# Norm weights that ride behind x transposed, ScalarE's first transfer, and two transfers for the first query weights

## The chip, the cores and the metric

One core of a Trainium2 chip runs the kernel once. The metric is the device time of one execution in microseconds (us). The kernel before has a median of 731.11 us in three runs (730.77 to 731.98).

## The reference

The kernel computes one decoder block on x of 512 tokens by 1,024 features in float32. The part that the change touches is the start: the norm of the input and the first projections.

```
h = x * rsqrt(mean(x*x) + EPS) * pre_mix_norm
[q_r, k_r, v_r, g_r, q_s, k_s, v_s, gate_r, gate_s] = h @ w_in
y_r = (silu(g_r) * GroupNorm(Retention_chunkwise(q_r, k_r, v_r))) @ w_ret_out
y_s = SWA_GQA_sinks_ALiBi(q_s, k_s, v_s) @ w_swa_out
x += RMSNorm((sigmoid(gate_r) * y_r + sigmoid(gate_s) * y_s) @ w_out) * post_mix_norm
x += RMSNorm(relu(RMSNorm(x) * pre_mlp_norm @ w_up)^2 @ w_down) * post_mlp_norm
```

## The kernel before

Every float32 matrix product is made of three products of rounded parts (`mm3`, lines 173 to 175): high by high, high by low, low by high. So each operand is split first: `split` (lines 129 and 130) writes the high part on ScalarE (ACT) and the rest on VectorE (DVE). TensorE (PE) does nothing but matmuls, 4,438 of them, in program order.

The start runs over KD = 8 blocks of 128 features. For each block k a transfer brings x transposed, `xTs[:, k]`, 128 partitions by 512 tokens, and another brings `raw_kv[:, k]`, the 256 columns of `w_in` that make sliding-window keys and values. `split_scaled` (lines 334 and 335) multiplies `xTs[:, k]` by the norm weight `gT[:, k]` of each feature and splits it into `xg`; `split` makes `wkv` of `raw_kv`. Then 12 matmuls per block add to four PSUM banks, `ptok`. The factor 1/rms of each token isn't known yet; it is put in later, as a row `R` (`factor_rows`, line 383 on PE and 385 on ACT), made of the squares of `xt`, x in its natural layout (line 354).

After the eight blocks come four `project_block`s of 24 matmuls each, with `pblk` as output: the sliding-window queries. Two of them use the weights of `raw_q` (a transfer of 1 MB, line 324), two those of a second pair (line 145). In the middle of the second block PE makes `R`. Then DVE scales the queries (line 408), makes the normed input out of `xTs`, `gT` and `R` (line 360), and ACT and DVE split it into `hT` (line 363 by way of `split`). The next `project_block` takes `hT` and the weights of `load_qk(0)`, two transfers of 512 KB in rows of 512 B (line 153): the retention queries and keys of head 0.

The order of work on each engine is set by a scheduler when the program is built; each engine then runs its own list strictly in order. Transfers are issued from three queues: SP's (`nc.sync`), ACT's (`nc.scalar`) and POOL's (`nc.gpsimd`, for transfers that add into a tile). SP's queue carries nearly all of the start. ACT's queue carries two: `gT` (128 partitions by 8 numbers) and `raw_kv` of block 0. In the list of ACT the split of `wkv` for block 1 stands ahead of that for block 0. `raw` tiles come from a ring of two buffers, so `raw_q` must be read before the transfers of `load_qk(0)` are issued.

Of the kernel before, what the change touches and what calls it, by code (L numbers as in the profile page):

```python
# [10 lines left out]
F32 = mybir.dt.float32  # L11
# [5 lines left out]
P = 128  # L17
D_MODEL = 1024
SEQ = 512
NT = SEQ // P  # L20
KD = D_MODEL // P
# [17 lines left out]
C_QR, C_KR, C_VR, C_GR, C_QS, C_KS, C_GATE_R = (0, 512, 1024, 2048, 3072, 3584, 3840)  # L39
# [47 lines left out]
    return np.ascontiguousarray(w.reshape(2, 4, P, 2, 512).transpose(3, 0, 2, 1, 4))  # L87


def f(ap):  # L90
    return ap.bitcast(F32)


@with_exitstack
def block_kernel(ctx, tc, x, xT, pre_mix, w_in, w_v, w_g, w_gate, w_ret, w_swa, w_out, sinks, post_mix,
                 pre_mlp, w_up, w_down, post_mlp, decay, chunk, dist, out):
    nc = tc.nc
    x, out = x[0], out[0]
    w_in, w_ret, w_swa, w_out = (w[0] for w in (w_in, w_ret, w_swa, w_out))
# [27 lines left out]
    def split(hi, lo, src):  # L127

        last["hi"] = nc.scalar.copy(hi, src)  # L129
        last["split"] = nc.vector.tensor_tensor(lo, src, f(hi), op=ALU.subtract)  # L130

    def raw_tile(shape):
        return stream.tile(shape, F32, name="raw", tag="raw", bufs=2)
# [49 lines left out]
    def wino_tokens(wx, b11, b12, b21, b22, f, dst):  # L183

        f11, f12, f21, f22 = f
        nc.vector.tensor_tensor(f11, f11, f12, op=ALU.subtract)
        split(dst[0][:, 0], dst[1][:, 0], f11)
        nc.vector.tensor_tensor(f12, f22, f12, op=ALU.subtract)
        split(dst[0][:, 2], dst[1][:, 2], f12)

        nc.vector.scalar_tensor_tensor(f22, f22, -1.0, f11, op0=ALU.mult, op1=ALU.subtract)
        split(dst[0][:, 1], dst[1][:, 1], f22)
        nc.vector.scalar_tensor_tensor(f21, f22, -1.0, f21, op0=ALU.mult, op1=ALU.subtract)
        split(dst[0][:, 3], dst[1][:, 3], f21)
        sums = [tuple(d[:, i] for d in dst) for i in range(4)]
        return {"11": b11, "21": b21, "22": b22, "t1": sums[0], "t2": sums[1],
                "t3": sums[2], "t4": sums[3]}
# [104 lines left out]
    side = ctx.enter_context(tc.tile_pool(name="side", bufs=1, side="right"))  # L302
    side.tile([P, 72], F32, name="pad")
    xTpool = sctx.enter_context(tc.tile_pool(name="xTpool", bufs=1, side="right"))
    xTs = xTpool.tile([P, KD, SEQ], F32, name="xTs", tag="xs")
    xgctx = ExitStack()
    xgpool = xgctx.enter_context(tc.tile_pool(name="xgpool", bufs=1, side="right"))
    gT = xgpool.tile([P, KD], F32, name="gT")
    xg = [xgpool.tile([P, KD, SEQ], F32R, name=f"xg{i}") for i in range(2)]
    xctx = ExitStack()  # L310
    xpool = xctx.enter_context(tc.tile_pool(name="xpool", bufs=1))
# [3 lines left out]
    nc.vector.memset(ones, 1.0)  # L315
    raw_kv = raw_tile([P, KD, 256])
    for k in range(KD):
        nc.sync.dma_start(xTs[:, k], xT[k])
        if k == 0:
            nc.scalar.dma_start(gT, pre_mix)  # L320
        queue = nc.scalar if k == 0 else nc.sync
        queue.dma_start(raw_kv[:, k], w_in[k * P : (k + 1) * P, C_KS : C_KS + 256])
    raw_q = raw_tile([P, KD, 256])
    nc.sync.dma_start(raw_q, w_in[:, C_QS : C_QS + 256].rearrange("(k p) c -> p k c", p=P))
    xts = [xpool.tile([P, D_MODEL], F32, name="xt", bufs=NT) for _ in range(NT)]
    for t in range(NT):
        nc.sync.dma_start(xts[t], x[t * P : (t + 1) * P, :])
# [4 lines left out]
    def split_scaled(hi, lo, src, scale):  # L332

        nc.scalar.mul(hi, src, scale)
        nc.vector.scalar_tensor_tensor(lo, src, scale, f(hi), op0=ALU.mult, op1=ALU.subtract)
# [620 lines left out]
    for half in range(2):  # L956
# [11 lines left out]
        with tc.high_priority(offset=CHAIN_AHEAD):  # L968
            for t in range(2):
# [4 lines left out]
                for n in range(2):  # L974
                    c = slice(n * 512, (n + 1) * 512)
# [152 lines left out]
    def left(j, q):  # L1128
        hi, lo = (ring.tile([P, 4, 256], F32R, name=f"left{i}") for i in range(2))
        split(hi, lo, uc[j][:, q])  # L1130
        return hi, lo

    def right(src):
        return [parts(src[:, 2 * i : 2 * i + 2], [P, 2, 512]) for i in range(2)]
# [141 lines left out]
    for j in range(2):  # L1276
        a, b = left(j, 3), right(tch[j])
# [21 lines left out]
    for i in range(2):  # L1299
        c = slice(i * 256, (i + 1) * 256)  # L1300
# [9 lines left out]
    residual(3, factor(3), [(512, outz[3])] + zs)  # L1310


_INS = ['x', 'xT', 'pre_mix_norm', 'w_in', 'w_v', 'w_g', 'w_gate', 'w_ret_out', 'w_swa_out', 'w_out', 'sinks', 'post_mix_norm',
        'pre_mlp_norm', 'w_up', 'w_down', 'post_mlp_norm']


# [28 lines left out]
```

## Time and profile before

| what | value |
|---|---|
| median of the runs shown | 731.11 us |
| the profiled execution's own time | 731.96 us |
| its span, first to last instruction | 730.2 us |
| PE busy | 718.1 us, 98% of the span |
| DVE busy | 535.6 us, 73% |
| ACT busy | 423.8 us, 58% |
| mean granted TensorE clock | 0.997 |
| bytes moved by transfers | 117.79 MB, 161 GB/s mean |

The profiled execution's time and its span differ by 1.8 us, which lies around the instructions. A row of a timeline gives the start, the duration, the engine, the line of the kernel, the operation, the output and inputs, and behind it in brackets how long the engine was idle before and what ended that. An engine name with a q (SPq, ACTq) marks the issue of a transfer, not the transfer.

### The profile page before, as it was taken

What the parts mean: (1) busy time and instruction counts of PE and PEld (TensorE: products, weight loads), DVE (VectorE), ACT (ScalarE), POOL (GpSimd) and SP (SyncE); (2) the same over time, 40 slices, a digit from 0 to 9 for tenths busy, and PEclk for the clock granted to TensorE, in tenths of its full rate; (3) what the DMA queues carried; (4) which work ended last, traced back from release to release, by engine and by line L of the source; (5) the groups of instructions that cost most, each with busy time, mean ns of one, the idle gap of its engine ahead of it and who ended that gap; (6) DMA issues with size and microseconds to landing.
All of it is one profiled execution on the core that took longest, in us unless ns stands there. A gap on an engine that the chain in (4) does not pass through costs nothing.

```text
span 730.2 us, 11250 instructions
## 1 busy us (share of the span) xinstructions
PE 718.1 (98%) x4438; PEld 640.3 (88%) x4438; DVE 535.6 (73%) x808; ACT 423.8 (58%) x714; POOL 60.5 (8%) x75
## 2 busy tenths in 40 slices
PE   8999999999999999999999999999999999999996
PEld 8877878888888999989888999999999888888885
DVE  5699976677975756566944866677676788987797
ACT  6667676445665534435634865766667756555571
POOL 0200000211100000000011101100000010010010
PEclk9999999999999999999999999999999999999998
DMA  9954434907444446543661619766753899698603
GB/s 314 331 170 85 104 83 144 289 4 145 87 144 117 143 117 179 151 133 115 216 247 58 160 49 283 198 172 169 197 147 117 266 291 238 156 203 200 116 0 116
DMA packets 43749, 117.79 MB, mean 161 GB/s; under 512 B 3504, under 2 KB 21296, under 8 KB 37552
## 3 DMA queue, kind: packets, MB, share of 16 engines
q1 hardware_dynamic: 36928, 80.76, 31.5%
q0 software_dynamic: 6480, 36.18, 26.4%
q8 instruction: 35, 0.57, 0.3%
q10 hardware_dynamic: 288, 0.14, 0.1%
q14 instruction: 18, 0.15, 0.1%
HBM read 114.96 MB, written 2.10 MB: 160 GB/s over the span
## 4 chain that ended last, share of the span: by engine, by line
PE 67%; DVE 5%; DMA 2%; issue 1%; ACT 1%; POOL 1%; POOLq 0%; DVEq 0%; ACTq 0%
PE wino L173 10%; PE wino L174 10%; PE wino L175 10%; PE p L174 5%; PE p L173 5%; PE p L175 5%; PE yr L173 2%; PE yr L174 2%; PE ps L174 2%; PE yr L175 2%; PE ps L175 2%; PE ps L173 2%; DVE wlo L130 2%; PE up L175 2%; PE up L174 2%; PE up L173 2%
## 5 line engine op out<-in xcount | busy, mean ns | idle before, releaser
L130 DVE TENSOR_TENSOR wlo<-raw,whi 128x1024 fp32r<-128x1024 f32 x81 | 98.6, 1222 | 49.6 <-ACT whi L129 49.6
L129 ACT CAST whi<-raw 128x1024 fp32r<-128x1024 f32 x81 | 84.7, 1051 | 41.4 <-DMA raw<-in_w_down 7.5
L174 PE MATMUL p<-wlo,left 128*128 128x512 f32 x216 | 84.2, 390 | 0.0
L175 PE MATMUL p<-whi,left 128*128 128x512 f32 x216 | 84.1, 390 | 0.0
L173 PE MATMUL p<-whi,left 128*128 128x512 f32 x216 | 84.0, 390 | 0.1
L175 PEld LDWEIGHTS p<-whi,left 128*128 128x128 f32 x216 | 40.5, 188 | 9.1 <-DVE left L130 0.8
L174 PEld LDWEIGHTS p<-wlo,left 128*128 128x128 f32 x216 | 40.6, 188 | 8.7 <-DVE wlo L130 0.3
L173 PEld LDWEIGHTS p<-whi,left 128*128 128x128 f32 x216 | 40.5, 188 | 8.8 <-ACT left L129 0.5
L130 DVE TENSOR_TENSOR wlo<-tch,whi 128x1024 fp32r<-128x1024 f32 x32 | 38.6, 1219 | 7.5 <-ACT whi L129 7.5
L129 ACT CAST left<-uc 128x1024 fp32r<-128x1024 f32 x28 | 29.3, 1052 | 23.2 <-PE p L174 23.2
L130 DVE TENSOR_TENSOR left<-uc,left 128x1024 fp32r<-128x1024 f32 x28 | 34.1, 1220 | 10.2 <-ACT left L129 10.2
L129 ACT CAST p<-rs 128x1024 fp32r<-128x1024 f32 x21 | 22.0, 1050 | 31.2 <-DVE rs L224 31.2
L129 ACT CAST whi<-tch 128x1024 fp32r<-128x1024 f32 x32 | 33.2, 1050 | 11.7 <-PE p L175 6.8
L130 DVE TENSOR_TENSOR p<-rs,p 128x1024 fp32r<-128x1024 f32 x21 | 25.7, 1225 | 14.7 <-ACT p L129 14.7
L130 DVE TENSOR_TENSOR wlo<-rs,whi 128x1024 fp32r<-128x1024 f32 x21 | 25.7, 1224 | 10.5 <-ACT whi L129 8.4
L173 PE MATMUL wino<-h2c,whi 128*128 128x256 f32 x104 | 29.4, 283 | 0.0
L174 PE MATMUL wino<-h2c,whi 128*128 128x256 f32 x104 | 29.4, 283 | 0.0
L175 PE MATMUL wino<-h2c,wlo 128*128 128x256 f32 x104 | 29.4, 283 | 0.0
L174 PE MATMUL wino<-h2s,p 128*128 128x256 f32 x104 | 29.4, 283 | 0.0
L175 PE MATMUL wino<-h2s,p 128*128 128x256 f32 x104 | 29.4, 283 | 0.0
L173 PE MATMUL wino<-h2s,whi 128*128 128x256 f32 x104 | 29.4, 283 | 0.0
L174 PE MATMUL wino<-h2s,whi 128*128 128x256 f32 x104 | 29.4, 283 | 0.0
(350 smaller groups left out, 2328.7 us busy)
## 6 DMA issues: line engine op xcount, KB each, us to landing
tch<-in_w_down POOLq DMA_DIRECT2D x12, 1024.0 KB, 9.6
raw<-in_w_down SPq DMA_DIRECT2D x7, 1024.0 KB, 7.6
rs<-in_w_up SPq DMA_DIRECT2D x13, 512.0 KB, 4.1
rs<-in_w_up POOLq DMA_DIRECT2D x13, 512.0 KB, 5.4
raw<-in_w_up SPq DMA_DIRECT2D x13, 512.0 KB, 5.1
raw<-in_w_in SPq DMA_DIRECT2D x8, 512.0 KB, 5.3
acc<-in_w_v POOLq DMA_DIRECT2D x4, 1024.0 KB, 8.0
rs<-in_w_gate SPq DMA_DIRECT2D x8, 512.0 KB, 3.7
```

The source lines that it names most:

```text
L129: last["hi"] = nc.scalar.copy(hi, src)
L130: last["split"] = nc.vector.tensor_tensor(lo, src, f(hi), op=ALU.subtract)
L173: nc.tensor.matmul(ps, ah, bh, start=first, stop=False, skip_group_check=more)
L174: nc.tensor.matmul(ps, ah, bl, start=False, stop=False, skip_group_check=more)
L175: nc.tensor.matmul(ps, al, bh, start=False, stop=last, skip_group_check=more)
```

## The change

Three edits, all in the first loads:

- The norm weights are no longer an input of their own. On the host each block of x transposed gets two more columns, both holding the norm weight of the feature, so a row is 514 numbers (2,056 B) where it was 512 (2,048 B). `xTs` and `gT` become views of the wider tile `xT_in`. The transfer of `gT` on ACT's queue is gone.
- With it gone, `raw_kv` of block 0 is the first and only transfer on ACT's queue.
- `raw_q` is loaded in two transfers of 128 columns each (rows of 512 B) where it was one transfer of 256 columns (rows of 1 KB).

```diff
+def norm_blocks(x, gain):
+
+    return np.concatenate([x.T, gain[:, None], gain[:, None]], 1).reshape(KD, P, SEQ + 2)
...
-    xTs = xTpool.tile([P, KD, SEQ], F32, name="xTs", tag="xs")
+
+    xT_in = xTpool.tile([P, KD, SEQ + 2], F32, name="xTs", tag="xs")
+    xTs = xT_in[:, :, :SEQ]
+    gT = xT_in[:, :, SEQ]
...
-    gT = xgpool.tile([P, KD], F32, name="gT")
...
     for k in range(KD):
-        nc.sync.dma_start(xTs[:, k], xT[k])
-        if k == 0:
-            nc.scalar.dma_start(gT, pre_mix)
+        nc.sync.dma_start(xT_in[:, k], xT[k])
         queue = nc.scalar if k == 0 else nc.sync
         queue.dma_start(raw_kv[:, k], w_in[k * P : (k + 1) * P, C_KS : C_KS + 256])
     raw_q = raw_tile([P, KD, 256])
-    nc.sync.dma_start(raw_q, w_in[:, C_QS : C_QS + 256].rearrange("(k p) c -> p k c", p=P))
+    for b in range(2):
+        c0 = C_QS + b * P
+        nc.sync.dma_start(
+            raw_q[:, :, b * P : (b + 1) * P],
+            w_in[:, c0 : c0 + P].rearrange("(k p) c -> p k c", p=P),
+        )
```

On ACT, at the very start, the list before is this (`raw_111` is `raw_kv`, `wkv0_108` and `xg0_102` are the high parts; a wait named DMAHW is one for a transfer):

```order
L320 DMA gT_101<-in_pre_mix_norm 128x8
L115 ACT_TABLE_LOAD
L115 ACTIVATE early_74<-mhalf_72 128x4 [waits DVE_49]
L322 DMA raw_111<-in_w_in 128x256
L334 ACTIVATE xg0_102<-xTs_97,gT_101 128x512 [waits DMAHW1_49,DMAHW0_49]
L334 ACTIVATE xg0_102<-xTs_97,gT_101 128x512 [waits DMAHW2_49]
L129 CAST wkv0_108<-raw_111 128x256 [waits DMAHW3_49]
L129 CAST wkv0_108<-raw_111 128x256 [waits DMAHW4_49]
```

Here the two `xg` of blocks 0 and 1 go ahead of the two `wkv`, and of these block 1 goes ahead of block 0. The list of the changed kernel at the same place:

```order
L327 DMA raw_110<-in_w_in 128x256
L120 ACT_TABLE_LOAD
L120 ACTIVATE early_74<-mhalf_72 128x4 [waits DVE_49]
L134 CAST wkv0_107<-raw_110 128x256 [waits DMAHW0_49]
L344 ACTIVATE xg0_101<-xTs_97 128x512 [waits DMAHW1_49]
L344 ACTIVATE xg0_101<-xTs_97 128x512 [waits DMAHW2_49]
L134 CAST wkv0_107<-raw_110 128x256 [waits DMAHW3_49]
```

The `wkv` split of block 0 has moved ahead of both `xg`, and that of block 1 stands behind them. DVE's list has the same shift: the low part of `wkv` for block 0 first, then two of `xg`, then block 1's.

On SP's queue the rows around `raw_q` before (`raw_129` is `raw_q`, `raw_405` the second pair of query weights, `acc_454` the retention values' weights, `raw_509` the weights of `load_qk(0)`):

```order
L324 DMA raw_129<-in_w_in 128x8x256
L327 DMA xt_131<-in_x 128x1024
L327 DMA xt_132<-in_x 128x1024
L327 DMA xt_133<-in_x 128x1024
L327 DMA xt_134<-in_x 128x1024
L145 DMA raw_405<-in_w_in 128x8x256
L597 DMA acc_454<-in_w_v 128x2048
L599 DMA acc_454<-in_w_v 128x2048
L153 DMA raw_509<-in_w_in 128x8x128 x2
```

And in the changed kernel:

```order
L331 DMA raw_127<-in_w_in 128x8x128 x2
L337 DMA xt_130<-in_x 128x1024
L337 DMA xt_131<-in_x 128x1024
L337 DMA xt_132<-in_x 128x1024
L337 DMA xt_133<-in_x 128x1024
L150 DMA raw_404<-in_w_in 128x8x256
L607 DMA acc_453<-in_w_v 128x2048
L609 DMA acc_453<-in_w_v 128x2048
L158 DMA raw_508<-in_w_in 128x8x128 x2
```

Only the first row differs, two transfers where one was; what follows keeps its order. PE's and POOL's lists are unchanged, and ACT's later list differs only in one `kv` copy (line 395) that now stands ahead of the last square of `xt`.

## Rows read from the trace of the kernel before

**Rows 1.** The longest waits of PE over the whole span: who waited for whom, us in total, times, longest.

```profile
PE ptok L173 <- ACT wkv L129: 1.5, 1, 1.5
PE warm L330 <- POOL ident masks.py:199: 1.4, 1, 1.4
PE pblk L175 <- DVE wlo L130: 0.8, 1, 0.8
PE swa_s L424 <- ACT vg L631: 0.7, 1, 0.7
```

**Rows 2.** Busy time by engine in the stretch from 3 to 33.5 us: length, busy us (instructions) of PE, PEld, DVE, ACT and POOL, granted clock, mean busy share of the 16 DMA engines, GB/s.

```profile
3.00:33.50 30.50, 28.92 (x176) 25.67 (x175) 19.01 (x34) 20.51 (x35) 5.14 (x9) 1.00 1.06 353
```

**Rows 3.** Timeline of ACT in the first 6 us, its issues of transfers among it.

```profile
0.74 0.40 ACTq L320 DMA_DIRECT2D gT<-in_pre_mix_norm  x1
1.24 0.39 ACTq L322 DMA_DIRECT2D raw<-in_w_in  x1
...
3.72 1.50 ACT L334 ACTIVATE xg<-xTs,gT 128x512 fp32r<-128x512 f32 x2 [1.05 <-DMA gT<-in_pre_mix_norm]
5.47 0.71 ACT L129 CAST wkv<-raw 128x256 fp32r<-128x256 f32 x2 [0.24 <-DMA raw<-in_w_in]
```

**Rows 4.** Timeline of DVE at the same place.

```profile
4.47 1.53 DVE L335 SCALAR_TENSOR_TENSOR xg<-xTs,gT,xg 128x512 fp32r<-128x512 f32 x2 [3.44 <-ACT xg L334]
6.21 0.76 DVE L130 TENSOR_TENSOR wkv<-raw,wkv 128x256 fp32r<-128x256 f32 x2 [0.20 <-ACT wkv L129]
```

**Rows 5.** Timeline of PE: the warm-up matmuls, the first three matmuls on data, the first of the first query block, and the eight that make R.

```profile
1.37 3.36 PE L330 MATMUL warm<-ident 128*128 128x128 f32 x14 [1.37 <-POOL ident masks.py:199]
6.23 0.38 PE L173 MATMUL ptok<-wkv,xg 128*128 128x256 f32 x1 [1.50 <-ACT wkv L129]
...
6.92 0.28 PE L175 MATMUL ptok<-wkv,xg 128*128 128x256 f32 x1
...
18.18 0.40 PE L173 MATMUL pblk<-xg,whi 128*128 128x512 f32 x1
...
26.59 1.05 PE L383 MATMUL R<-diag,ones 128*128 128x128 f32 x8
```

**Rows 6.** Issues on SP's queue: the first two blocks of x transposed, raw_kv of block 1, raw_q, and the two transfers of load_qk(0).

```profile
0.74 0.84 SPq L318 DMA_DIRECT2D xTs<-in_xT  x2
1.64 0.42 SPq L322 DMA_DIRECT2D raw<-in_w_in  x1
...
8.57 0.38 SPq L324 DMA_DIRECT2D raw<-in_w_in  x1
...
19.85 2.27 SPq L153 DMA_DIRECT2D raw<-in_w_in  x2
```

**Rows 7.** Issues with their size and the time from the start of the issue to the landing, each from a narrow stretch: block 0 of x transposed (issued at 0.74), raw_kv of block 0 (1.24) and of block 1 (1.64), raw_q (8.57), the first transfer of load_qk(0) (19.85).

```profile
xTs<-in_xT SPq DMA_DIRECT2D x1, 256.0 KB, 2.8
...
raw<-in_w_in ACTq DMA_DIRECT2D x1, 128.0 KB, 3.5
...
raw<-in_w_in SPq DMA_DIRECT2D x1, 128.0 KB, 3.8
...
raw<-in_w_in SPq DMA_DIRECT2D x1, 1024.0 KB, 7.8
...
raw<-in_w_in SPq DMA_DIRECT2D x1, 512.0 KB, 11.5
```

**Rows 8.** Packets in four stretches: 12.5 to 14.0 us (rows of 1 KB of raw_q, and three of 4 KB), 28.8 to 30.4 us (rows of 512 B of load_qk(0)), 16.5 to 18.5 us (rows of 4 KB of xt), and ACT's queue (q10) from 2.3 to 33.5 us: packets, MB, share of 16 engines. The smallest packets, counted under 512 B in the first three, are the marks that end a transfer.

```profile
DMA packets 517, 0.54 MB, mean 358 GB/s; under 512 B 2, under 2 KB 514, under 8 KB 517
...
DMA packets 929, 0.48 MB, mean 298 GB/s; under 512 B 14, under 2 KB 928, under 8 KB 928
...
DMA packets 221, 0.80 MB, mean 401 GB/s; under 512 B 28, under 2 KB 28, under 8 KB 220
...
q10 hardware_dynamic: 288, 0.14, 1.5%
```

**Rows 9.** Timeline of ACT from 31 to 36 us: the high parts of the weights of load_qk(0) (128x1024) and of the normed input hT (128x512).

```profile
31.39 1.05 ACT L129 CAST whi<-raw 128x1024 fp32r<-128x1024 f32 x1 [3.11 <-DMA raw<-in_w_in]
...
33.57 1.05 ACT L129 CAST whi<-raw 128x1024 fp32r<-128x1024 f32 x1 [0.62 <-DMA raw<-in_w_in]
34.53 1.14 ACT L129 CAST hT<-xTs 128x512 fp32r<-128x512 f32 x2
```

**Rows 10.** Timeline of DVE from 32 to 43.4 us; between the last two rows it has no idle time.

```profile
32.98 0.69 DVE L130 TENSOR_TENSOR hT<-xTs,hT 128x512 fp32r<-128x512 f32 x1 [0.97 <-ACT hT L129]
35.17 1.29 DVE L130 TENSOR_TENSOR hT<-xTs,hT 128x512 fp32r<-128x512 f32 x2 [1.50 <-ACT hT L129]
...
42.10 1.22 DVE L130 TENSOR_TENSOR wlo<-raw,whi 128x1024 fp32r<-128x1024 f32 x1
```

**Rows 11.** Timeline of PE at the first block on hT.

```profile
42.22 0.39 PE L174 MATMUL pblk<-hT,whi 128*128 128x512 f32 x1
43.37 0.50 PE L175 MATMUL pblk<-hT,wlo 128*128 128x512 f32 x1 [0.76 <-DVE wlo L130]
```

**Rows 12.** PE's last matmul, and the granted clock (the number ahead of the last two) in two stretches after it.

```profile
722.74 0.28 PE L175 MATMUL p4c<-whi,left 128*128 128x256 f32 x1
...
724.00:725.70 1.70, 0.00 (x0) 0.00 (x0) 0.84 (x3) 0.51 (x2) 0.55 (x1) 0.94 0.04 12
725.70:730.20 4.50, 0.00 (x0) 0.00 (x0) 1.35 (x3) 0.00 (x0) 0.00 (x0) 0.50 0.33 117
```

More of the change, by code (lines that the diff above doesn't have):

```diff
@@ L94, in block_kernel @@
 @with_exitstack
-def block_kernel(ctx, tc, x, xT, pre_mix, w_in, w_v, w_g, w_gate, w_ret, w_swa, w_out, sinks, post_mix,
+def block_kernel(ctx, tc, x, xT, w_in, w_v, w_g, w_gate, w_ret, w_swa, w_out, sinks, post_mix,
                  pre_mlp, w_up, w_down, post_mlp, decay, chunk, dist, out):
@@ L1310, in block_kernel @@
     residual(3, factor(3), [(512, outz[3])] + zs)
-_INS = ['x', 'xT', 'pre_mix_norm', 'w_in', 'w_v', 'w_g', 'w_gate', 'w_ret_out', 'w_swa_out', 'w_out', 'sinks', 'post_mix_norm',
+_INS = ['x', 'xT', 'w_in', 'w_v', 'w_g', 'w_gate', 'w_ret_out', 'w_swa_out', 'w_out', 'sinks', 'post_mix_norm',
         'pre_mlp_norm', 'w_up', 'w_down', 'post_mlp_norm']
@@ L1325 @@
         inputs, w_in=w_in[:, :, :C_GATE_R],
-        xT=np.asarray(inputs["x"])[0].T.reshape(KD, P, SEQ),
-        pre_mix_norm=np.asarray(inputs["pre_mix_norm"]).reshape(KD, P).T,
+        xT=norm_blocks(np.asarray(inputs["x"])[0], np.asarray(inputs["pre_mix_norm"])[0]),
         w_v=wide_blocks(w_in[0, :, C_VR:C_GR]),
```

## The prediction

> **What bounds the kernel now.** I began with PE's waits, since PE is busy for 98% of the span. The list is short [rows 1]: 1.5 us for the first matmul on data, 1.4 us for the warm-up's operand, 0.8 us for a weight split by DVE, 0.7 us for a copy by ACT, nothing longer. A gain at the start therefore lives only if none of the later waits takes it back, and the question is what ends each of them.
>
> The first wait: `ptok` starts at 6.23 [rows 5]. It needs `wkv` and `xg` of block 0. ACT makes the two `xg` first, from 3.72, when `gT` has landed, and then at 5.47 the first `wkv`, behind a transfer [rows 3]. That transfer is block 1's: it was issued at 1.64 [rows 6] and landed 3.8 us later [rows 7], at 5.44. Block 0's weights had landed at 1.24 + 3.5 = 4.74 [rows 3, 7], but their split stands second and ends at 5.47 + 0.71 = 6.18, just ahead of PE. PE then goes on without a break from its third matmul at 6.92 [rows 5].
>
> The third wait: PE's first block on `hT` issues two matmuls and stops; the third comes at 43.37, after 0.76 us idle, when DVE has written `wlo` at 42.10 + 1.22 = 43.32 [rows 10, 11]. Followed back, DVE has no idle time from 35.17 to there [rows 10], so its end is fixed at 35.17. At 35.17 it waited 1.50 us for ACT's `hT`; ACT makes that at 34.53, strictly behind a weight split that starts at 33.57, when the second transfer of `load_qk(0)` lands [rows 9]. And from 3 to 33.5 us the 16 DMA engines are full: share 1.06 at 353 GB/s [rows 2]. `load_qk(0)`'s first transfer was issued at 19.85 and landed 11.5 us later [rows 6, 7], most of which is queueing. So the chain that bounds this stage is the sum of all packets ahead of 33.57, then ACT, then 8.15 us of DVE, then PE. PE's own start isn't on it.
>
> **The change part by part.**
>
> *Weights first on ACT's queue, with the new order of the splits.* Without `gT`, block 0's weights are issued at 0.74 where it was 1.24 [rows 3]. They share the engines with block 0 of x, which landed at 0.74 + 2.8 = 3.5 alone [rows 7]; its 8 rows of 1 KB per engine add 0.37 (priced below), so for both together I estimate 3.9. ACT then splits `wkv` (0.71 for two, 0.36 each) and `xg` (1.50 for two, 0.75) of block 0: done at 3.9 + 0.36 + 0.75 = 5.0. DVE's low part of `xg` takes 1.53 / 2 = 0.77 [rows 4], so the third matmul may start at 5.85 where it was 6.92. PE's start moves ahead by about 1.05 us. The ends: nothing, if the shared landing takes all of it, and 1.05. I take 1.0; it doesn't enter the sum, as said below.
>
> *Two transfers for the first queries.* Once PE is 1.0 us ahead, its first query block comes at 17.2 instead of 18.18 [rows 5], and `raw_q` as a whole landed at 8.57 + 7.8 = 16.4 [rows 6, 7]; split on ACT and DVE (1.05 and 1.22, as in rows 9 and 10) its low part would be there at 18.6 only. The first half alone should land some 2 us earlier, so this edit covers the first. Its price is in packets. Rows of 1 KB: 24 us of engine time (1.5 us on 16 engines), less three 4 KB packets at 32 us / 192 = 0.167, over 512 packets is 45.9 ns each. Rows of 512 B: 25.6 us over 914 is 28.0 ns [rows 8]. Per engine `raw_q` cost 64 x 45.9 = 2.94 us and will cost 128 x 28.0 = 3.58 us: **+0.65 us** of full DMA time ahead of 33.57. Nothing hides it there, since the engines have no free time.
>
> *Wider rows of x.* 1,024 rows, 64 per engine, of 2,056 B. Between 1 KB (45.9 ns) and 4 KB (167 ns) a byte costs 0.039 ns, so 8 bytes cost 0.3 ns and all rows 0.02 us. If the 8 bytes go as a packet of their own, they cost what a small packet costs. ACT's queue held 288 packets for 1.5% of 16 x 31.2 us, 7.49 us [rows 8]; less 128 rows of 1 KB (5.88) that leaves 1.61 us over 160 small ones, 10 ns each, and 64 x 10 = 0.64 us. I take the lower end, +0.02, as the rows of all sizes lie near one line, and keep 0.64 for the range.
>
> No row here shows transfers whose rows start off a round address. [...]
>
> *`gT` gone.* 128 small packets of 10 ns over 16 engines: -0.08 us.
>
> *The rest.* DVE and ACT read the same number of elements at another row pitch, at no cost; one `kv` copy ahead of the last square costs ACT the same total.
>
> **Sum.** The landing that fixes DVE moves by +0.65 + 0.02 - 0.08 = +0.6 us, and DVE's `wlo` and PE's third matmul move with it, to 43.97. PE gets there 1.0 us earlier and waits 0.76 + 1.0 + 0.6 = 2.4 us instead of 0.76. What it gained at the start is given back here, and what the packets cost is left: +0.6 us. Later loads are issued when work frees their buffers, so they move along. The profiled execution of 731.96 us would take 732.6; the median of 731.11 becomes **731.7**. Bounds: +0.5 (no cost for wide rows, rows of 512 B 0.1 us cheaper) to +1.3 (both upper ends). If block 0's weights land no earlier, the change doesn't do what it says at the start, yet the sum is the same.
>
> **The rivals.**
>
> *The landing follows the issue.* The two transfers of `load_qk(0)` are issued when DVE has read the last of `raw_q`, at 19.85. In the changed kernel the second half lands near 17.0, and ACT and DVE need 1.05 + 1.22 for it: 19.25. If the engines' share above 1 only counts waiting packets, and the queue could be served faster, then the landing comes 0.6 us earlier, DVE too, and so the end: 730.5. For it: shares above 1.0 can't be work alone. Against it: 11.5 us between issue and landing.
>
> [...]
>
> *The wide rows break up (slower).* If 2,056 B go as four pieces of 512 B and one small one, a row costs 4 x 28 + 10 = 122 ns against some 85 on the line above: 64 x 37 = 2.4 us, with the rest +3.0: 734.1. Nothing in the rows speaks for it but the odd size.
>
> **How the numbers follow.** A measurement of this kernel can tell about 0.2%, 1.46 us, from no change. The forecast, +0.5 to +1.3, gets 0.64; the landing that follows the issue 0.12; the clock 0.12; broken rows 0.08; 0.04 stays for a gain that is kept whole together with the 0.76 us (729.4). The range takes in the first three, from 730.3 to 733.3, and leaves out 0.12. Faster by over 0.2%: 0.05. Slower: 0.12 + 0.08, and 0.01 of the forecast's upper end, 0.21. Within: 0.74.
>
> **What would show it.** Right: `ptok`'s first matmuls near 5 to 6 us; packets of `raw_q` at 28 ns; the second weight split of `load_qk(0)` on ACT near 34.2 instead of 33.57; PE's wait for `wlo` in the first block on `hT` near 2.4 us, and its end near 44. Wrong: that wait ending before 43.37 (the landing follows the issue, or DVE isn't bound by it); matmuls 0.45 us apart behind it (the clock); rows of x above 100 ns each. If DVE had idle time between 35 and 43 us in the new trace, the chain that I read would not be the one that binds.

## The result, and the profile after

The changed kernel takes 733.49 us (median of ten runs, 732.94 to 734.28) against 731.52 us for the kernel before (ten runs): a ratio of 1.0027, interval 1.0018 to 1.0035. It is 1.97 us slower. The forecast was +0.6 us with a range up to 733.3, so the sign of the sum is right, its size is not, and the time lies outside the range. The profiled execution took 733.44 us; its span and PE's busy time, from the head of the page:

```profile
span 731.7 us, 11251 instructions
...
PE 721.4 (99%) x4438; PEld 642.0 (88%) x4438; DVE 536.0 (73%) x808; ACT 423.9 (58%) x714; POOL 60.2 (8%) x75
```

The span of before was 730.2 us, with 718.1 us of PE. The same 4,438 matmuls now keep PE busy for 3.3 us longer: 2.0 us of it in `ptok` (14.04 us against 12.04) and 1.8 us in `yr` and `ys`, as shown below. No wait explains the loss: among the longest waits of PE after the change (answering to [rows 1]) none has grown, and the wait for `wlo`, of which the forecast made its 2.4 us, isn't there.

```profile
PE warm L340 <- POOL ident masks.py:199: 1.4, 1, 1.4
PE swa_s L434 <- ACT vg L641: 0.7, 1, 0.7
PE ptok L178 <- ACT xg L344: 0.4, 1, 0.4
```

**The start.** ACT (as in [rows 3]) and PE (as in [rows 5]) after the change:

```profile
0.74 0.40 ACTq L327 DMA_DIRECT2D raw<-in_w_in  x1
...
4.04 0.40 ACT L134 CAST wkv<-raw 128x256 fp32r<-128x256 f32 x1 [1.37 <-DMA raw<-in_w_in]
4.35 1.33 ACT L344 ACTIVATE xg<-xTs 128x512 fp32r<-128x512 f32 x2
```

```profile
5.12 0.58 PE L178 MATMUL ptok<-wkv,xg 128*128 128x256 f32 x1 [0.40 <-ACT xg L344]
...
5.90 0.58 PE L180 MATMUL ptok<-wkv,xg 128*128 128x256 f32 x1
...
6.71 0.41 PE L180 MATMUL ptok<-wkv,xg 128*128 128x256 f32 x1
6.92 0.41 PE L178 MATMUL ptok<-wkv,xg 128*128 128x256 f32 x1
...
11.17 0.28 PE L178 MATMUL ptok<-wkv,xg 128*128 128x256 f32 x1
11.28 0.28 PE L179 MATMUL ptok<-wkv,xg 128*128 128x256 f32 x1
...
18.99 0.39 PE L178 MATMUL pblk<-xg,whi 128*128 128x512 f32 x1
```

The weights of block 0 land 3.3 us after an issue at 0.74, `ptok` starts at 5.12 instead of 6.23, and its third matmul at 5.90 instead of 6.92: the 1.0 us are there. But matmuls of 256 columns then start 0.21 us apart until about 10.8, and 0.11 us apart from there. That is read here as a lower clock: the spacing is near twice, and the trace's own record of the granted clock begins at 10.87 us, with a share of 1.00 (at the end of the program it falls to 0.50, at 727.67). (The windowed view prints 1.00 for the stretch ahead of 10.87 too, so the spacing is what tells of that time.) So `pblk` starts at 18.99, 0.81 us later than before.

**The first block on `hT`.** ACT from 31 to 36 us, DVE and PE, answering to [rows 9 to 11]:

```profile
32.01 1.05 ACT L134 CAST whi<-raw 128x1024 fp32r<-128x1024 f32 x1 [2.95 <-DMA raw<-in_w_in]
32.96 0.61 ACT L134 CAST hT<-xTs 128x512 fp32r<-128x512 f32 x1
33.60 1.05 ACT L134 CAST whi<-raw 128x1024 fp32r<-128x1024 f32 x1
34.56 1.14 ACT L134 CAST hT<-xTs 128x512 fp32r<-128x512 f32 x2
```

```profile
35.21 1.29 DVE L135 TENSOR_TENSOR hT<-xTs,hT 128x512 fp32r<-128x512 f32 x2 [0.91 <-ACT hT L134]
...
42.13 1.22 DVE L135 TENSOR_TENSOR wlo<-raw,whi 128x1024 fp32r<-128x1024 f32 x1
```

```profile
43.37 0.39 PE L179 MATMUL pblk<-hT,whi 128*128 128x512 f32 x1
43.60 0.40 PE L180 MATMUL pblk<-hT,wlo 128*128 128x512 f32 x1
```

The first transfer of `load_qk(0)` lands 0.62 us later (31.39 to 32.01). The second weight split starts at 33.60, as in the kernel before (33.57), yet now without idle time ahead of it: ACT comes to it from the chain behind the first transfer, and the second has just landed, at 19.60 + 13.9 = 33.5. The issues on SP's queue, of both transfers (the first at 18.25) and of the second alone, and the second's time to the landing (as in [rows 6, 7]):

```profile
18.25 8.77 SPq L158 DMA_DIRECT2D raw<-in_w_in  x2
...
19.60 7.42 SPq L158 DMA_DIRECT2D raw<-in_w_in  x1
```

```profile
raw<-in_w_in SPq DMA_DIRECT2D x1, 512.0 KB, 13.9
```

DVE's `wlo` stands at 42.13 (42.10 before). PE's third matmul comes at 43.60 instead of 43.37, with no wait: PE itself is as late as that. So up to here the change costs about 0.2 us in this pair of profiles.

**Where the time went.** PE's matmuls that write `yr` (the retention output projection) and `ys` (the same for the sliding window): duration min/median/max in ns, first and last start in us. First the kernel before, then the changed one.

```profile
L174 PE MATMUL ys<-swaT,whi x32: 387/389/396, 206.9 to 230.2; 128*128 128x512 f32 x32
L174 PE MATMUL yr<-retT,whi x64: 389/389/398, 252.4 to 355.8; 128*128 128x512 f32 x64
```

```profile
L179 PE MATMUL ys<-swaT,whi x32: 393/394/398, 206.7 to 230.6; 128*128 128x512 f32 x32
L179 PE MATMUL yr<-retT,whi x64: 394/394/396, 252.8 to 357.4; 128*128 128x512 f32 x64
```

At the first of these `ys` the changed kernel is 0.2 us ahead, at the last 0.4 behind, at the first `yr` 0.4, at the last 1.6 us behind, and at the last matmul of all, 724.21 against 722.74 in [rows 12], 1.47. Every single one of these matmuls takes about 5 ns more, the smallest and the median alike: it is no wait, it is a slower matmul. Three of `yr` in a row in the timeline, before and after:

```profile
252.84 0.40 PE L173 MATMUL yr<-retT,whi 128*128 128x512 f32 x1
253.07 0.39 PE L174 MATMUL yr<-retT,whi 128*128 128x512 f32 x1
253.31 0.39 PE L175 MATMUL yr<-retT,wlo 128*128 128x512 f32 x1
253.53 0.39 PE L173 MATMUL yr<-retT,whi 128*128 128x512 f32 x1
...
254.21 0.39 PE L173 MATMUL yr<-retT,whi 128*128 128x512 f32 x1
```

```profile
253.28 0.39 PE L178 MATMUL yr<-retT,whi 128*128 128x512 f32 x1
...
254.68 0.39 PE L178 MATMUL yr<-retT,whi 128*128 128x512 f32 x1
```

Six matmuls from 252.84 to 254.21 are 0.228 us each; from 253.28 to 254.68, 0.233. Summed over the tile (busy time of PE with its count behind the length of the stretch; first row `yr`, second `ys`):

```profile
0.00:731.00 731.00, 44.28 (x192) 35.79 (x192) 5.50 (x8) 1.00 0.58 161
0.00:731.00 731.00, 22.49 (x96) 17.88 (x96) 10.92 (x16) 4.61 (x8) 1.00 0.58 161
```

```profile
0.00:731.00 731.00, 45.47 (x192) 35.66 (x192) 5.50 (x8) 1.00 0.59 161
0.00:731.00 731.00, 23.06 (x96) 17.83 (x96) 10.91 (x16) 4.60 (x8) 1.00 0.59 161
```

That is +1.19 and +0.57 us at a granted clock of 1.00. The matmuls of `pblk` that read `xg` went from 389 to 394 ns as well; those of `pblk` on `hT`, of `wide` and of `ps`, of the same 512 columns, did not move. What `xg`, `swaT` and `retT` have in common is that they are the moving operand and lie in the right-hand stack of SBUF. The built program tells how they moved: the wider tile of x is 64 B longer in each partition (8 rows of 8 B), so all that is allocated behind it in that stack starts 64 B lower. Before, every operand of TensorE but `ident` started at 192 modulo 256; after, those of the right-hand stack start at 128.

### The profile page after: what moved, and what is told of

Read it like the earlier page. It is cut to its first block, busy times and chain, and to the rows that moved or that the text cites. A ratio compares the mean times of both kernels' runs of the same rounds, so it can differ in the third digit from the quotient of the medians.

```text
span 731.7 us, 11251 instructions
## 1 busy us (share of the span) xinstructions
PE 721.4 (99%) x4438; PEld 642.0 (88%) x4438; DVE 536.0 (73%) x808; ACT 423.9 (58%) x714; POOL 60.2 (8%) x75
## 4 chain that ended last, share of the span: by engine, by line
PE 67%; DVE 5%; DMA 2%; issue 1%; ACT 1%; POOL 1%; POOLq 0%; DVEq 0%; ACTq 0%
PE wino L180 10%; PE wino L179 10%; PE wino L178 10%; PE p L178 5%; PE p L180 5%; PE p L179 5%; PE yr L178 2%; PE yr L180 2%; PE yr L179 2%; PE ps L178 2%; PE ps L180 2%; PE ps L179 2%; DVE wlo L135 2%; PE up L178 2%; PE up L180 2%; PE up L179 2%
```

## The experiments

Two theories stood at first. A: the time goes to the places of the moving operands. B: it goes to the start, to packets and the lower clock. The experiments use the filler tile that both kernels have at the head of the right-hand stack (72 numbers), which costs nothing but its space. In the expectations a place "64 mod 128" is 192 modulo 256, and "0" is 128 (in e8 also 64, and 0).

**e1, the changed kernel with its tiles where they were.**

```
-    side.tile([P, 72], F32, name="pad")
+    side.tile([P, 56], F32, name="pad")
```

> The changed kernel with the filler tile ahead of x transposed cut from 72 to 56 numbers, so that every tile of the right-hand stack (xg, swaT, retT, the retention tiles) stands again where it stood in the kernel before, while the wider x, the new first transfer and the two halves of the query weights stay. Theory A (the time is lost because these tiles moved by 64 B: matmuls that stream a tile that starts at a multiple of 128 B take 233 ns instead of 227): the yr and ys matmuls go back to 227 ns, 288 x 6.2 ns = 1.8 us come back, ratio to before 0.999 to 1.001. Theory B (the time is lost in the start, by packets and by PE's first matmuls at the lower clock): nothing changes by the move, ratio 1.0020 to 1.0035, yr and ys stay at 233 ns.

732.25 us, ratio 0.9999 [0.9979, 1.0018]. `yr` is back at 44.28 us and `ys` at 22.49, though its start had the lower clock until 11 us like the changed kernel (12 matmuls in the stretch from 8 to 10 us and 11 in the changed kernel, where the kernel before has 19). 16 numbers less of filler take back the loss. The interval alone would leave room for a part of it; the rows of `yr` and `ys` decide. A stands.

**e2, the kernel before with its tiles where the change put them**: the same line with 88.

> The kernel before with the filler tile grown from 72 to 88 numbers and nothing else: the right-hand stack stands 64 B lower, as in the changed kernel. Theory A: slower by 1.5 to 2 us, ratio 1.0020 to 1.0030, yr and ys at 233 ns, and ptok, whose stationary operand is xg, faster (114 instead of 120 ns). Theory B: ratio 0.9995 to 1.0005.

733.18 us, 1.0018 [1.0009, 1.0027]; `yr` 45.47, `ys` 23.06. The places alone, without a packet or an issue changed, make most of the loss (1.0018 of 1.0027): A from the other side.

**e4, half that way**: the kernel before with 80, tiles at 160 modulo 256.

> The kernel before with the filler at 80 numbers: the right-hand stack starts 32 B lower, at 32 past a multiple of 128 B. Theory A in the form that only a start at a multiple of 128 B costs: ratio 0.9995 to 1.0005 and yr at 227 ns. In the form that any start but 64 past a multiple costs: yr above 227 ns and a ratio above 1.0015. Theory B: no change.

733.0 us, 1.0022 [1.0007, 1.0037], `yr` 45.43. Half the distance costs as much.

**e7, one tile alone**: the kernel before with 64 B behind `retT` in its pool, so that `retT` moves and no other operand.

```
     retT = [apool.tile([P, KD, SEQ], F32R, name=f"retT{i}") for i in range(2)]
+    apool.tile([P, 16], F32, name="pad2")
```

> The kernel before with 64 bytes of filler behind retT, so that retT alone among the operands of TensorE starts at 0 mod 128. By the theory of the moving operand's place the 192 matmuls of yr run 233 ns apart instead of 227, 44.83 us instead of 43.63, and nothing else changes: +1.2 us at the end of that stage, which nothing behind it takes back, 732.7. If the places matter only by what lies beside a tile in the same pool or by the load on the start, yr stays at 227 and the time at 731.5.

`yr` 45.47 us, `ys` 22.49 as before: only the matmuls that read the moved tile are slower. The median, 732.63, is 0.96 us up, but the interval [0.9988, 1.0023] doesn't exclude no change; the verdict rests on the rows of `yr` and `ys`:

```profile
0.00:731.00 731.00, 45.47 (x192) 35.67 (x192) 5.50 (x8) 1.00 0.58 161
0.00:731.00 731.00, 22.49 (x96) 17.87 (x96) 10.91 (x16) 4.60 (x8) 1.00 0.58 161
```

**e3, e5 and e6, the two transfers.** e3 is e1 with `raw_q` in one transfer again, e5 the changed kernel with one, e6 the kernel before with two:

```
-    for b in range(2):
-        c0 = C_QS + b * P
-        nc.sync.dma_start(
-            raw_q[:, :, b * P : (b + 1) * P],
-            w_in[:, c0 : c0 + P].rearrange("(k p) c -> p k c", p=P),
-        )
+    nc.sync.dma_start(raw_q, w_in[:, C_QS : C_QS + 256].rearrange("(k p) c -> p k c", p=P))
```

> As e1, but the first query weights come in one transfer again (rows of 1 KB). My forecast's packet term: the first transfer of the next weights lands 0.6 us earlier than in e1; since the second was not what DVE waited for in the changed kernel, theory A expects the end within 0.3 us of e1. A theory in which the packets of the split cost the time expects it 0.6 us or more faster than e1. The first query block may now wait for its low part of the weights, near 18 us.

> The changed kernel with raw_q in one transfer again and nothing else undone: its tiles of the right-hand stack stay where the change put them (0 mod 128). If the cost of the two transfers is the 0.65 us that the prediction worked out, the time falls from 733.49 to 732.8; if it is the 1.2 us by which e3 was below e1, to 732.3. By either yr, ys and pblk on xg stay at 233 ns apart. Rival: the two transfers cost nothing by themselves and e3 was faster for its early clock; then 733.5.

> The kernel before with raw_q in two transfers and nothing else: all tiles stay at 64 mod 128, so matmuls stay 227 ns apart. Here PE is not ahead, its wait for wlo at 43 us is there to grow. By the packets +0.65 us, 732.2; by e3 against e1 +1.2 us, 732.7; by the rival that the transfers cost nothing 731.5.

e3: 731.01, 0.9989 [0.9979, 0.9998]. e5: 732.94, 1.0025 [1.0013, 1.0038]. e6: 731.77, 1.0000 [0.9990, 1.0011]. For e6 the interval doesn't exclude the +0.65 us of the packets either. The interval of e3 lies just below 1: the new first transfer with the old places and one load may be worth up to 0.2%, though e10, with the same start, doesn't show it. The transfers' price should be seen where it arises, at the first weights of `load_qk(0)` on ACT. In e5, with one transfer:

```profile
30.95 1.06 ACT L134 CAST whi<-raw 128x1024 fp32r<-128x1024 f32 x1 [1.95 <-DMA raw<-in_w_in]
```

and in e6, with two, where ACT begins the second split at 33.95:

```profile
32.33 1.05 ACT L129 CAST whi<-raw 128x1024 fp32r<-128x1024 f32 x1 [2.72 <-DMA raw<-in_w_in]
...
33.95 1.05 ACT L129 CAST whi<-raw 128x1024 fp32r<-128x1024 f32 x1
```

Against 32.01 of the changed kernel, e5 is 1.06 us earlier; against 31.39 of before [rows 9], e6 0.94 later. But each of these is one execution, and the same row of e1, with two transfers, and of e8, with one, stands the other way round:

```profile
31.48 1.05 ACT L134 CAST whi<-raw 128x1024 fp32r<-128x1024 f32 x1 [2.11 <-DMA raw<-in_w_in]
```

```profile
32.39 1.05 ACT L135 CAST whi<-raw 128x1024 fp32r<-128x1024 f32 x1 [4.25 <-DMA raw<-in_w_in]
```

Over all twelve profiles that row starts at 31.48 to 32.44 with two transfers (four profiles, mean 32.07) and at 30.95 to 32.39 with one (eight, mean 31.43). The means differ by 0.64 us, near the 0.65 that was forecast, but the ranges overlap, and the kernels differ in other things too. ACT's second split and DVE's `wlo` are later by 0.54 each in the same means (33.63 against 33.10, 42.16 against 41.63). What of it reaches the end isn't shown: in the changed start the medians differ by 0.55 (e5 against the changed kernel) and 1.24 us (e3 against e1), and the intervals of these pairs overlap; in e6 the time does not move. Between nothing and 1.2 us is what can be said.

**e8, the stationary operand.** `ptok` had become faster: its median matmul takes 276 ns where others of 256 columns take 283, and in it the stationary operand `xg` had moved, the moving `wkv` had not. e8 is e3 with the split weights that PE holds put at another place. `placed` makes the tile 32 numbers longer and uses it from number `at` on, 16 where it is the stationary operand, 0 where it is the moving one; the shorter filler moves the right-hand stack by 128 B, from 192 to 64 modulo 256, which is the same place modulo 128:

```
+HELD = 16
-        hi = stream.tile(shape, F32R, name="whi", tag="whi")
-        lo = stream.tile(shape, F32R, name="wlo", tag="wlo")
+        hi = placed(stream, shape, "whi", at, tag="whi")
+        lo = placed(stream, shape, "wlo", at, tag="wlo")
...
-    side.tile([P, 56], F32, name="pad")
+    side.tile([P, 24], F32, name="pad")
```

> The changed kernel with one load of raw_q and its old places (e3), and in it the split weights that TensorE holds as its stationary operand (whi and wlo, not p24 and p22) start at 0 mod 128, all moving operands at 64. In the changed kernel ptok, whose stationary operand alone had moved to 0, ran 114 ns apart instead of 120, and the ret products 118. If the stationary operand's place counts by itself, the wino products on whi and wlo (about half of those, some 880 matmuls of 256 columns) run 2 to 6 ns closer, 1.8 to 5.3 us less: 726 to 729 against 731.0 of e3. If ptok ran closer for another reason (its moving operand wkv, or both on different places), nothing changes: 731.0.

729.95 us, 0.9977 [0.9965, 0.9988], the fastest of all. It fell between the expectations, and its rows told why the theory was too simple. `wino`, the matmuls of 256 columns, in e3 and then in e8:

```profile
0.00:731.00 731.00, 212.94 (x1764) 212.38 (x1764) 32.02 (x63) 30.56 (x84) 1.00 0.58 161
```

```profile
0.00:731.00 731.00, 208.59 (x1764) 207.95 (x1764) 31.95 (x63) 30.10 (x84) 1.00 0.59 161
```

They gain 4.35 us. But `yr` lost 0.80 (45.08) and `wide` 0.9: the tiles 128 B longer had moved the next buffers too, so that the weights start at 0 and at 128 modulo 256 in turn. The moving operand of `yr` starts at 64 throughout. Where the next weights start at 0, its matmuls are 229.5 ns apart (63 of them), and where they start at 128, 233.4 (64). A place of the moving operand that is good or bad in itself doesn't fit that; the distance from the moving to the stationary operand does.

**e9, everything moved alike.** The changed kernel with nothing undone; 192 B of filler on the left-hand side bring all operands to 128 modulo 256, at distance 0 again.

```
     ident = const.tile([P, P], F32, name="ident")
+    const.tile([P, 48], F32, name="pad_left")
-    side.tile([P, 72], F32, name="pad")
+    side.tile([P, 8], F32, name="pad")
```

> The changed kernel, nothing undone, with 192 bytes of filler ahead of the left-hand stack and 256 bytes less on the right: every operand of TensorE, moving and stationary, now starts at 128 mod 256, where the changed kernel has its right-hand tiles. If the spacing goes by the distance between moving and stationary operand (0 mod 256: 227 ns at 512 columns, 120 at 256), as the eight runs together read, yr, ys and pblk on xg are back at 227 and the time is that of e1, 732.25. If it goes by where the moving operand lies itself (192 mod 256 good, the others bad), all matmuls of 512 columns now run 233 apart, some 1,700 x 6 ns = 10 us more: 742 to 744.

731.62 us, 1.0006 [0.9997, 1.0015]. `yr` and `ys`, which stand at the places where they were slow, and the last matmul:

```profile
0.00:731.00 731.00, 44.28 (x192) 35.79 (x192) 5.50 (x8) 1.00 0.58 161
0.00:731.00 731.00, 22.48 (x96) 17.87 (x96) 10.93 (x16) 4.61 (x8) 1.00 0.58 161
```

```profile
722.79 0.28 PE L181 MATMUL p4c<-whi,left 128*128 128x256 f32 x1
```

722.79 against 722.74 in [rows 12]: the whole loss of the profiled execution but 0.05 us is gone. So for the 512 columns of `yr` and `ys` it is the distance, not the place. The change without it measures +0.06%, with an interval from -0.03% to +0.15%; the forecast of +0.6 us, 0.08%, lies inside, and so does no change at all.

**e10, the distance put to use.** e3 with the moving operands of the up projection 64 B further away.

```
+    h2pool.tile([P, 16], F32, name="pad_h2")
     h2c = [h2pool.tile([P, 2, 4, 256], F32R, name=f"h2c{i}") for i in range(2)]
...
+    rspool.tile([P, 48], F32, name="pad_rs")
...
+    ppool.tile([P, 16], F32, name="pad_h2b")
```

> e3 (the changed kernel with its old places and one load of raw_q) with 64 bytes of filler ahead of the tiles that hold the second norm's output (h2b, h2c, h2d, h2s) and 192 behind them: the moving operands of the 1,092 or so matmuls of 256 columns in the up projection lie 64 bytes further from their stationary operands, all else as in e3. If the distance counts, these run 115 ns apart where it was 120: 1,092 x 5 ns, 5.5 us less, 725.5. If e8 was faster for another reason (the longer slots of its stream tiles), 120 ns and 731.0. If TensorE then waits for the weights' splits on VectorE or ScalarE, which it now overtakes, between the two.

731.97 us, 1.0008 [0.9996, 1.0020]: a miss. The matmuls are faster, by half of what was expected (median 279 to 280 ns instead of 283), and the 1,092 of the up projection's pairs take 128.77 us of PE instead of 131.36. Waits that e3 doesn't have stand against it:

```profile
PE p L178 <- ACT left L134: 1.1, 1, 1.1
...
PE up L178 <- ACT h2c L134: 0.7, 1, 0.7
PE up L178 <- DVE zg L981: 0.6, 1, 0.6
```

The first is the down projection, which PE reaches earlier than ACT has split its first operand. Those at the head of the up projection (401 us) come ahead of any faster matmul; what makes them no run shows. PE's last matmul comes 0.38 us earlier than in e3's profile, but the ratio to the kernel before is 1.0008 where e3 had 0.9989: it is no improvement that can be shown.

## Why the prediction failed, step by step

**The step that failed is "the rest": "DVE and ACT read the same number of elements at another row pitch, at no cost".** The wider rows were followed to DMA, DVE and ACT, and not to the allocator. Eight bytes in each of eight rows moved every later tile of the right-hand stack by 64 B, and with them the moving operands of 384 matmuls. Of these 288 count (`yr` 1.19 and `ys` 0.57 us, 1.76 of the 1.97 us); the 96 of `pblk` on `xg` lie ahead of 43 us, where PE had 0.76 us to spare before. A little comes back, as `ret_v` runs some 3 ns faster. e9, e1 and e2 show this cause three times over; e7 shows it on one tile.

**PE's earlier start: right by itself, and lost otherwise.** The third matmul of `ptok` came at 5.90; 5.85 was forecast (the terms given for it add up to 5.78). In the changed kernel's profile the gain was lost to the lower clock, not to a wait of 2.4 us. Where the upper level comes early, the forecast of this part is met: in e3 the first query block starts at 17.25 (17.2 forecast), PE's second matmul on `hT` at 41.09 where it was 42.22, and PE then waits for `wlo`, 1.09 us instead of 0.76.

```profile
17.25 0.40 PE L178 MATMUL pblk<-xg,whi 128*128 128x512 f32 x1
...
42.57 0.50 PE L180 MATMUL pblk<-hT,wlo 128*128 128x512 f32 x1 [1.09 <-DVE wlo L135]
```

That the change brings the late clock isn't shown: of the twelve profiles, the upper level came by 6.3 us in two of seven with the new start (e3 and e8) and three of five with the old one. e2 and e6 had the old start and matmuls at the lower level until after 10 us (12 and 11 in the stretch from 8 to 10 us, where e3 has 19). What sets it stays open.

**The packets: not refuted, and the size not settled.** +0.65 us was forecast for the split of `raw_q`. The sign that was named, packets at 28 ns, is near: in the changed kernel from 12.5 to 14.0 us some 908 rows of 512 B pass, 26 ns each by the forecast's own working, which would make +0.4 us.

```profile
DMA packets 925, 0.47 MB, mean 313 GB/s; under 512 B 16, under 2 KB 924, under 8 KB 925
```

The landing of the first transfer moved by 0.62 in the pair of before and after, and by 0.64 in the means over the twelve profiles. Since profiles with the same transfers differ by 1.0 to 1.4 us, the close agreement is in part luck.

**The chain from the landing to PE: its binder was read from one profile.** The forecast took the second transfer's landing as what fixes ACT, from the 0.62 us of idle time ahead of the second split [rows 9]. In the eleven other profiles, the changed kernel's among them, that idle time is 0.07 us or less: the second transfer lands up to 0.2 us ahead of the moment when ACT comes free from the chain behind the first. In the pair of before and after the second landing stays at 33.5, so of the +0.6 us nothing is seen at DVE (42.13 against 42.10); but the 42.10 of before is late among the eight profiles with one transfer (41.01 to 42.55, mean 41.63). So neither end of the forecast wait of 2.4 us came: PE arrived later than 41.6, and DVE ended at 42.13 + 1.22 = 43.35, before 43.97.

**The other rivals.** The landing did not follow the issue: the two transfers of `load_qk(0)` were issued at 18.25, 1.6 us earlier than before, and the first landed 0.62 us later. For a clock that falls in a longer wait, which had a chance of 0.12 and stands behind the upper end of the range, 733.3, no run shows a case: no wait of PE there grew to 2.4 us. What is shown is the end of the program: before, the granted clock falls from 1.00 to 0.50 at 725.5 (0.94 in the mean from 724.0 to 725.7 [rows 12]), 2.5 us after PE's last matmul ended, and in the changed kernel 3.2 us after; over the twelve profiles it is 2.0 (e2) to 4.8 us (e7). The wide rows did not break up: the trace holds 1,024 packets of 2,056 B, 96.0 ns each in the mean, where the 2,048 B of before took 95.1, and nothing of +3.0 us is there once the operands are in line (e9). Over all profiles the means are 93.9 to 99.1 ns for the wide rows and 91.3 to 95.1 for the others, some 3 ns apart or 0.2 us in all, more than the 0.02 us taken. How much of the 3 ns comes from the length of the rows, and how much from where they start, no run here tells apart. The upper bound of +1.3 was 0.1 us more than its terms add up to, which changes nothing.

## What to carry to other kernels

When a tile grows by some bytes, look at the start of every tile behind it, in the built program, before you count packets; a filler that restores the old places (in e1 `yr` was back at 44.28 us from 45.47, and the ratio at 0.9999) separates "what the edit does" from "where it shifted things". When matmuls of one tile are slower by the same few ns in minimum and median and others of the same shape are not (here `yr`, 389 to 394 ns in both, and not `wide`), it is no wait and no clock: compare the places of their operands. And a faster matmul is only worth what the engines that feed it can follow, as e10's waits of 1.1, 0.7 and 0.6 us suggest. Last, a chain that was read from one profile can be that execution's own: read the same rows in a second one before you say what binds.

## What was not expected of the hardware

With fp32r operands the time from one matmul to the next depends on how far apart its moving and stationary operands start within a partition: for 512 columns by the rows of e1, e2, e7 and e9. From the starts in the traces of before, after, e2, e4, e7 and e8, matmuls whose weights change with each one, by distance (moving less the next stationary start, modulo 256 B), mean ns from start to start:

| distance | 512 columns | 256 columns |
|---|---|---|
| 0 | 227.3 (5,335) | 119.9 (7,917) |
| 32 | none | 117.2 (115) |
| 64 | 229.6 (200) | 115.0 (639) |
| 128 | 232.9 (327) | 119.0 (105) |
| 192 | 233.4 (825) | 117.0 (433) |
| 224 | 233.1 (254) | none |

Distance 0 is the best for 512 columns and the worst for 256. At 256 columns it isn't the whole rule: 64 gave 113.8 ns in e8, where the moving operand starts at 192 and the stationary one at 128 (408 matmuls), but 117.8 in e10, where they start at 0 and 192 (919). What happens inside no run shows.
